# Attention probabilities: one exponential and a rounding copy on ACT, in place of two exponentials and some copies on DVE

## The chip, the core and the metric

The kernel runs on one core of one Trainium2 chip. The metric is the time of one launch in device microseconds; before the change the median of three runs is 2537.33 us (2531.2 to 2538.35). The engines are named as in the profile: PE is TensorE (matmul), with PEld for its weight loads; DVE is VectorE, ACT is ScalarE, POOL is GpSimd, SP is SyncE, which issues most of the DMAs. A row with `q` behind an engine's name (SPq) is that engine's sequencer.

## The reference, cut to what matters

Two layers, each a mixer with attention and a feed-forward block, on 1024 positions of width 1024, all in float32. Layer 0 has 12 causal heads of width 64 with a decay ("fox"), layer 1 has 12 causal heads of width 96 ("mla"); each layer adds 4 heads that look at 256 memory positions. In every head

```
logits = jnp.einsum('bhqd,bhkd->bhqk', qc, k).astype(jnp.float32)
logits = jnp.where(key_idx[None, :] <= q_idx[:, None], logits, -jnp.inf)
p = jax.nn.softmax(logits, axis=-1).astype(v.dtype)
return jnp.einsum('bhqk,bhkd->bhqd', p, v)
```

The probabilities `p` enter the second product. This is the place that the change touches.

## The kernel before, in words

PE multiplies values of the type float32r, which keeps fewer bits than float32. To keep the precision the kernel splits an operand into a high part (rounded to float32r) and a low part (the rest), and multiplies the parts apart. For the probabilities the high part is `ph`, the float32 value is `pf` and the low part `plo` is `pf - ph`.

Work goes head by head, and in a head by groups: a causal head has six groups of scores of 1024, 896 or 384 columns (two of each), a memory head has two of 1024. Each layer has 12 x 6 + 4 x 2 = 80 groups, the kernel 160. For each group:

- PE writes the transposed scores, with the row's maximum already subtracted by an extra row of the operands, into a PSUM tile `psS` (two buffers).
- `probs` turns them into `ph`, `pf` and `plo` (lines 329 to 341). In most groups ACT takes the exponential of `psS` twice, once rounded into `ph` (L335) and once in full into `pf` (L336). In every fifth group of layer 0 and every sixth of layer 1 (`pl.dve_turn`) ACT takes it once into `pf` (L338) and DVE rounds `pf` into `ph` (the helper `copy`, L85). POOL then subtracts (the helper `sub`, L90). `pf` has two buffers, `ph` and `plo` three.
- Two groups later PE multiplies `ph`, and one group after that `plo`, with the values (`av_units`), into the PSUM tile `psO` (one buffer). ACT copies `psO` out into `oh` (DVE does so for the memory heads of layer 0).

Beside this, PE, ACT and DVE prepare the next head: PE transposes into one of three `psX` tiles (L106), ACT scales them into `KA` and `QA` (L516), DVE makes the low parts `KB` and `QB` (L517), and DVE takes the maximum of a first pass over the scores (`mA`, L292 and L297), which PE also writes into `psX`. In layer 1 the queries and keys of a pair of heads are projected and normalised in the same stretch (`gq`, `gk`, `g_ss`, `rs_v`, `rs_y`, `rs_t` on DVE, `sq` and `rope` on POOL and DVE).

The code is not emitted in the order in which it runs. A scheduler that simulates the engines sets the order of each engine's list. In layer 0 it is free to move the matmuls of attention; in layer 1 they are pinned to the program's order (`pin[0] = not offset`), while ACT, DVE and POOL are free. All engines work through their lists in order, so an instruction that waits holds up all that stand behind it.

Of the kernel before, what the change touches and what calls it, by code (L numbers as in the profile page):

```python
# [11 lines left out]
AF = mybir.ActivationFunctionType  # L12
# [62 lines left out]
def hybrid_kernel(ctx: ExitStack, tc: tile.TileContext, A, out):  # L75
    nc = tc.nc
# [4 lines left out]
    def copy(eng, o, i):  # L81
        if eng == "a":
            nc.scalar.copy(o, i)  # L83
        elif eng == "v":
            nc.vector.tensor_copy(o, i)  # L85
        else:
            nc.gpsimd.tensor_copy(o, i)

    def sub(eng, o, a, b):
        (nc.vector if eng == "v" else nc.gpsimd).tensor_tensor(o, a, b, op=OP.subtract)  # L90
# [170 lines left out]

    pl = Pools()
    pl.mem_rows = set()
    pl.turn = 0

    def slot(name="slot", dt=F32):
        return pl.slots.tile([P, 1024], dt, name=name, tag="slot")
# [11 lines left out]
    def attention(L, heads, leads, offset=0, bg=None, fill={}):  # L279
# [30 lines left out]
        def score_units(h, g):  # L310
            half, parts = h.groups[g]
            state = {}

            def part(i):
                if i == 0:
                    state["ps"] = psS()
                ps = state["ps"]
                kt, q0, n, off = parts[i]
                passes = h.passes(kt, q0, n)
                for j, (l, r) in enumerate(passes):  # L320
                    mm(ps[:, off:off + n], l, r, j == 0, j == len(passes) - 1)
                if h.causal and q0 == kt * P:
                    mm(ps[:, off:off + P], idb, mS, False, True)
                if i == len(parts) - 1:
                    pend.append((h, g, *probs(ps, off + n)))

            return [lambda i=i: part(i) for i in range(len(parts))]

        def probs(ps, w):
            pf = pl.pf.tile([P, 1024], F32, name="pf")[:, :w]  # L330
            ph = pl.p.tile([P, 1024], F32R, name="ph")[:, :w]
            plo = pl.p.tile([P, 1024], F32R, name="plo", bufs=pl.nplo)[:, :w]
            pl.turn += 1
            if pl.turn % pl.dve_turn:
                nc.scalar.activation(ph, ps[:, :w], AF.Exp)  # L335
                nc.scalar.activation(pf, ps[:, :w], AF.Exp)  # L336
            else:
                nc.scalar.activation(pf, ps[:, :w], AF.Exp)  # L338
                copy("v", ph, pf)
            sub("p", plo, pf, ph.bitcast(F32))  # L340
            return ph, plo

# [134 lines left out]
    class Head:  # L477
# [6 lines left out]
        def qk_tiles(self):  # L484
            i = pl.nqk % len(pl.qk)
            pl.nqk += 1
            self.QA, self.KA, self.QB, self.KB = T = pl.qk[i]
            if self.causal and i not in pl.rows_set:
                pl.rows_set.add(i)
                for j, a, b in self.const_rows:  # L490
                    copy(self.rows_eng[len(pl.rows_set) > 1], T[j][a:b, :], ones1[a:b, 0:1].to_broadcast([b - a, S]))
# [873 lines left out]

    pl.split_out = split_out
    qk_tiles(qkp, (1, 2, 0), 3)
    pl.ev, pl.dve_turn = "v", 5
    fox = [FoxHead(h, QKV[h // 2][0], QKV[h // 2][1], cum) for h in range(NH)]
    mem = [MemHead(h, 0, mq0) for h in range(NMH)]  # L1370
    rest = attention(0, fox + mem, [2] * 16, offset=tc.cur_priority - p_last)
# [42 lines left out]
    with early(ffn.p_tail):  # L1414
# [4 lines left out]
        for d in range(ND):  # L1419
            raw = ffn.rp.tile([P, ND, P], F32, name="f_raw").rearrange("p a b -> p (a b)")[:, :N1 + N2]  # L1420
            nc.sync.dma_start(raw, mwin[d * P:(d + 1) * P, :])
            w = w1.tile([P, 2, N1 + N2], F32R, name="w1_w")
# [221 lines left out]
    def swap():  # L1644
# [3 lines left out]
        for p in (w1, xtp, hp):  # L1648
# [6 lines left out]

    fill = {2: [swap], 5: [lambda: g0.project(2)], 6: [lambda: latents_T(6)],
            10: [lambda: g0.project(3), lambda: g0.squares(1), lambda: g0.rotate(1), g0.scale_k, g0.scale_q]}
    pl.ev, pl.dve_turn = "a", 6
    mk = [slot("mK", F32R).rearrange("p (h i) -> p h i", h=NMH) for i in range(2)]

    ORDER = [12, 13, 14, 15, 0, 1, 2, 3, 4, 5, 6, 7, 8, 9, 10, 11]
# [98 lines left out]
```

## Time and profile before

| | us |
|---|---|
| median of 3 runs | 2537.33 |
| time of the profiled execution | 2535.55 |
| its span, first to last instruction | 2533.8 |
| attention of layer 0, stretch | 284 to 520 |
| attention of layer 1, stretch | 1397 to 1770 |
| PE busy in the span | 2372.8 |
| DVE busy in the span | 1905.2 |
| ACT busy in the span | 1208.7 |
| POOL busy in the span | 975.5 |

The two stretches are where `ph` is written and read (the first and the last use of it lie in them, with the preparation of the first head of layer 1). All else, the projections and the feed-forward blocks, holds no instruction of `probs`. Times of the rows below count from the start of the span.

### The profile page before, as it was taken

The page shows a single profiled execution, that of the slowest core. Times are in us where ns is not written, and L with a number is a line of the kernel's source. Part 1 is how long each engine was busy: PE and PEld are TensorE (multiplying, and loading weights), DVE is VectorE, ACT ScalarE, POOL GpSimd, SP SyncE. Part 2 cuts the span into 40 slices and gives each one's busy share as a digit, 9 for nine tenths or more (in the row PEclk, how much of TensorE's full clock was granted, in tenths as well). Part 3 has the DMA queues.
Part 4 walks back from the last instruction along what each step waited for, and adds up shares of the span by engine and source line. Part 5 has one row for each costly group of instructions (what it writes and reads, how often), then busy time and mean ns, then how long its engine had stood idle before and what let it go on. Part 6 is the DMA issues. An engine that isn't in the chain of part 4 may idle for free.

```text
span 2533.8 us, 32572 instructions
## 1 busy us (share of the span) xinstructions
PE 2372.8 (94%) x11609; PEld 1956.4 (77%) x11609; DVE 1905.2 (75%) x3289; ACT 1208.7 (48%) x2341; POOL 975.5 (38%) x640
## 2 busy tenths in 40 slices
PE   8999899988999999989998798989979999998999
PEld 7999666667788888868888576767768888886887
DVE  7432787737878877799997868874488778878998
ACT  5544678722544444434454555555144444443443
POOL 1122467732233333344322555666133233233442
PEclk9999899999999999999999899989999999999999
DMA  4221122262122222451230101011412222226221
GB/s 155 71 51 27 35 60 58 52 180 89 55 86 81 83 84 83 145 202 50 103 133 11 35 23 27 19 39 49 161 54 88 82 87 79 81 90 241 84 100 67
DMA packets 163652, 208.90 MB, mean 82 GB/s; under 512 B 11175, under 2 KB 124682, under 8 KB 163490
## 3 DMA queue, kind: packets, MB, share of 16 engines
q1 hardware_dynamic: 162054, 206.63, 25.9%
q8 instruction: 92, 1.51, 0.2%
q14 instruction: 70, 0.57, 0.1%
q10 hardware_dynamic: 1436, 0.18, 0.0%
HBM read 153.34 MB, written 39.98 MB: 76 GB/s over the span
## 4 chain that ended last, share of the span: by engine, by line
PE 71%; DVE 18%; DMA 4%; issue 3%; ACT 2%; POOL 1%; SPq 1%; DVEq 0%; ACTq 0%; POOLq 0%
PE psX L102 32%; PE psS L102 24%; PE psO L102 14%; DVE f_op L90 2%; DMA rrow<-rec 2%; PE psX L106 2%; DVE mA L292 1%; DVE psX L297 1%; DVE f_x L1134 1%; POOL f_op L90 1%; DVE rs_y L226 1%; DVE KB L517 1%; DVE QB L517 1%; DVE f_T L90 1%; DVE oh L93 1%
## 5 line engine op out<-in xcount | busy, mean ns | idle before, releaser
L90 POOL TENSOR_TENSOR f_op<-f_S,f_op 128x512 fp32r<-128x512 f32 x184 | 270.5, 1472 | 669.2 <-ACT f_op L83 612.0
L102 PE MATMUL psS<-f_T,f_op 128*128 128x512 f32 x1584 | 380.8, 391 | 5.4 <-DVE f_T L90 3.3
L90 POOL TENSOR_TENSOR plo<-pf,ph 128x1024 fp32r<-128x1024 f32 (+2 forms) x160 | 313.7, 1972 | 166.4 <-ACT pf L336 103.2
L102 PEld LDWEIGHTS psS<-f_T,f_op 128*128 128x128 f32 x1584 | 295.9, 188 | 66.9 <-DVE f_T L90 4.2
L102 PE MATMUL psX<-f_B,f_op 128*128 128x512 f32 x1260 | 296.3, 389 | 0.1
L83 ACT CAST f_op<-f_S 128x512 fp32r<-128x512 f32 x248 | 153.7, 621 | 279.5 <-PE psS L102 108.8
L102 PEld LDWEIGHTS psX<-f_B,f_op 128*128 128x128 f32 x1260 | 236.5, 188 | 49.6 <-issue 0.5
L102 PE MATMUL psS<-f_op 128*128 128x512 f32 x960 | 222.4, 390 | 0.4 <-DVE f_op L90 0.4
L102 PEld LDWEIGHTS psS<-f_op 128*128 128x128 f32 x960 | 180.6, 188 | 38.9 <-DVE f_op L90 1.2
L102 PE MATMUL psX<-f_op 128*128 128x512 f32 x666 | 174.5, 402 | 20.7 <-DVE f_op L90 18.0
L102 PE MATMUL psX<-w_w,hTh 128*128 128x384 f32 (+2 forms) x672 | 167.6, 334 | 2.2 <-ACT hTh L83 2.2
L102 PEld LDWEIGHTS psX<-f_op 128*128 128x128 f32 x666 | 127.3, 193 | 53.9 <-DVE f_op L90 24.4
L889 DVE SCALAR_TENSOR_TENSOR f_v<-f_cv,cw,f_v 128x1023 f32<-128x1023 f32 x88 | 151.0, 1715 | 7.6 <-ACT f_v L887 6.2
L83 ACT CAST f_op<-f_raw 128x512 fp32r<-128x512 f32 x148 | 91.4, 622 | 136.0 <-PE psS L102 70.7
L335 ACT ACTIVATE ph<-psS 128x1024 fp32r<-128x1024 f32 (+2 forms) x131 | 112.4, 858 | 89.6 <-PE psS L102 81.7
L102 PE MATMUL psX<-KA,QA 66*128 66x128 f32 (+4 forms) x320 | 111.4, 395 | 27.3 <-DVE mA L292 11.0
L83 ACT CAST f_op<-f_d 128x512 fp32r<-128x512 f32 x144 | 84.3, 619 | 102.0 <-PE psS L102 35.6
L849 DVE TENSOR_TENSOR f_u<-psS,f_p 128x512 f32<-128x512 f32 x44 | 30.4, 691 | 126.6 <-PE psS L102 126.6
L102 PEld LDWEIGHTS psX<-w_w,hTh 128*128 128x128 f32 x672 | 121.4, 190 | 3.3 <-ACT hTh L83 3.1
L102 PE MATMUL psS<-QA,KA 67*128 67x512 f32 (+7 forms) x304 | 111.4, 368 | 12.5 <-DMA QA<-mrow 12.4
L889 DVE SCALAR_TENSOR_TENSOR f_v<-f_cg,cw,f_v 128x1023 f32<-128x1023 f32 x88 | 112.7, 1280 | 10.9 <-ACT f_v L887 10.9
L90 POOL TENSOR_TENSOR f_op<-f_d,f_op 128x512 fp32r<-128x512 f32 x52 | 75.5, 1451 | 115.2 <-ACT f_op L83 115.2
(378 smaller groups left out, 5716.5 us busy)
## 6 DMA issues: line engine op xcount, KB each, us to landing
f_raw<-in_ffn_w_up_dram SPq DMA_DIRECT2D x88, 512.0 KB
g<-f_v SPq DMA_DIRECT2D x44, 512.0 KB
f_d<-g SPq DMA_DIRECT2D x36, 512.0 KB
f_d<-in_ffn_w_down_dram SPq DMA_DIRECT2D x36, 512.0 KB
w_raw<-in_fox_w_in_dram SPq DMA_DIRECT2D x48, 192.0 KB
rrow<-rec SPq DMA_DIRECT2D x32, 256.0 KB
wo_raw<-in_w_out_dram SPq DMA_DIRECT2D x32, 256.0 KB
xr<-x SPq DMA_DIRECT2D x16, 512.0 KB
```

The costliest lines, as they stand in the source:

```text
L83: nc.scalar.copy(o, i)
L90: (nc.vector if eng == "v" else nc.gpsimd).tensor_tensor(o, a, b, op=OP.subtract)
L93: (nc.vector if eng == "v" else nc.gpsimd).tensor_tensor(o, a, b, op=OP.mult)
L102: r = nc.tensor.matmul(*a, **k)
L106: r = nc.tensor.transpose(*a, **k)
L226: nc.vector.scalar_tensor_tensor(y, t, 1.5, y, op0=OP.add, op1=OP.mult)
L292: nc.vector.tensor_reduce(mA[:, q0:q0 + n], px[:, :n * width].rearrange("p (a b) -> p a b", a=n), axis=AX, op=OP.max)
L297: nc.vector.tensor_tensor_reduce(px[:, off:off + nk], px[:, off:off + nk], mQ[:, 512 - nk:], scale=1.0, scalar=m if on else NEG, op0=OP.ad ...
L335: nc.scalar.activation(ph, ps[:, :w], AF.Exp)
L517: nc.vector.scalar_tensor_tensor(Tl[tl0:tl1, hs], px, gcol, Th[0:n, hs].bitcast(F32), op0=OP.mult, op1=OP.subtract)
L849: nc.vector.tensor_tensor(o, x, y, op=OP.add)
L889: nc.vector.scalar_tensor_tensor(v[:, k:], src[:, :S - k], cw[:, 2 - k, ch:ch + 1], v[:, k:], op0=OP.mult, op1=OP.add)
```

## The change

`probs` takes one exponential into `pf` in every group, and ACT copies `pf`, rounded, into `ph`. The turn counter goes, and with it the copies on DVE. The later lines of the file move up by one to five: L335, L336 and L338 become L333, L516 becomes L511, L517 becomes L512, L297 becomes L296.

```diff
@@ -261,7 +261,6 @@
     pl = Pools()
     pl.mem_rows = set()
-    pl.turn = 0
@@ -330,13 +329,9 @@
             pf = pl.pf.tile([P, 1024], F32, name="pf")[:, :w]
             ph = pl.p.tile([P, 1024], F32R, name="ph")[:, :w]
             plo = pl.p.tile([P, 1024], F32R, name="plo", bufs=pl.nplo)[:, :w]
-            pl.turn += 1
-            if pl.turn % pl.dve_turn:
-                nc.scalar.activation(ph, ps[:, :w], AF.Exp)
-                nc.scalar.activation(pf, ps[:, :w], AF.Exp)
-            else:
-                nc.scalar.activation(pf, ps[:, :w], AF.Exp)
-                copy("v", ph, pf)
+
+            nc.scalar.activation(pf, ps[:, :w], AF.Exp)
+            copy("a", ph, pf)
             sub("p", plo, pf, ph.bitcast(F32))
             return ph, plo
@@ -1365,7 +1360,7 @@
-    pl.ev, pl.dve_turn = "v", 5
+    pl.ev = "v"
@@ -1655,7 +1650,7 @@
-    pl.ev, pl.dve_turn = "a", 6
+    pl.ev = "a"
```

Since a scheduler sets the lists, the change also moves other instructions. On PE the lists differ in the attention of layer 0 and in the last heads of layer 1; the feed-forward blocks and the first projections keep theirs. The first place is PE's list at the start of layer 0's attention, where `psS` takes the scores and `psO` the products with the probabilities of the first group:

```order
 L102 MATMUL psX<-KA_3076,QA_3075 128x512
-L102 MATMUL psO<-ph,vh 65x512
-L102 MATMUL psO<-ph,vl 64x512
-L102 MATMUL psO<-ph,vh 65x384
-L102 MATMUL psO<-ph,vl 64x384
+L102 MATMUL psS<-QB_3085,KB_3086 128x512
+L102 MATMUL psS<-QA_3083,KA_3084 128x512
+L102 MATMUL psS<-QB_3085,KB_3086 128x512
+L102 MATMUL psS<-QA_3083,KA_3084 128x512
 L102 MATMUL psS<-QB_3085,KB_3086 128x512
 L102 MATMUL psS<-QA_3083,KA_3084 128x512
```

The products of the first group with `ph` moved behind the scores of the next two groups.

The second place is ACT's list in layer 1, where a head's group of 896 columns falls beside the preparation of the next head (`KA_12777` and `QA_12776` are that head's operands). Before:

```order
L516 ACTIVATE QA_12776<-psX,g_cols 96x512
L335 ACTIVATE ph<-psS 128x896
L336 ACTIVATE pf<-psS 128x896
L516 ACTIVATE KA_12777<-psX,g_cols 96x512
L516 ACTIVATE QA_12776<-psX,g_cols 96x512
L338 ACTIVATE pf<-psS 128x384
```

And now:

```order
L511 ACTIVATE QA_12776<-psX,g_cols 96x512
L333 ACTIVATE pf<-psS 128x896
L511 ACTIVATE KA_12777<-psX,g_cols 96x512
L83 CAST ph<-pf 128x896
L511 ACTIVATE QA_12776<-psX,g_cols 96x512
L333 ACTIVATE pf<-psS 128x384
L83 CAST ph<-pf 128x384
```

The rounding copy stands behind `KA`, one instruction later than the second exponential stood.

The third place is DVE's list a little later in the same head, behind the low part `QB`, where the maximum over 128 columns is followed by the Newton steps of a norm (`rs_y`, `rs_t`). Before:

```order
L517 SCALAR_TENSOR_TENSOR QB_12778<-psX,g_cols,QA_12776 96x512
L297 ISA psX,mA<-psX,mQ 128x128
L297 ISA mA 128x1
L85 CAST ph<-pf 128x384
L217 TENSOR_SCALAR rs_y<-rs_v 128x16
```

And now:

```order
L512 SCALAR_TENSOR_TENSOR QB_12778<-psX,g_cols,QA_12776 96x512
L296 ISA psX,mA<-psX,mQ 128x128
L296 ISA mA 128x1
L217 TENSOR_SCALAR rs_y<-rs_v 128x16 x2
```

The copy is gone, and nothing took its place.

## Rows read from the trace of the kernel before

**Rows 1.** The page: chain that ended last, shares of the span by engine.
```profile
PE 71%; DVE 18%; DMA 4%; issue 3%; ACT 2%; POOL 1%; SPq 1%; DVEq 0%; ACTq 0%; POOLq 0%
```

**Rows 2.** Stretches: us, busy PE, PEld, DVE, ACT, POOL (instructions), clock, DMA, GB/s.
```profile
284.00:520.00 236.00, 216.49 (x1168) 156.64 (x1168) 186.33 (x357) 179.72 (x263) 170.23 (x90) 0.95 0.23 54
1397.00:1770.00 373.00, 327.01 (x1848) 253.29 (x1848) 274.66 (x615) 205.97 (x313) 227.67 (x148) 0.92 0.12 31
```

**Rows 3.** PE's longest wait for an engine, layer 0, then 1: us, times, longest.
```profile
PE psX L106 <- DVE mA L297: 8.3, 7, 2.2
...
PE psX L102 <- DVE mA L292: 9.2, 6, 3.9
```

**Rows 4.** Stretches as in rows 2, only instructions that touch the tile ph.
```profile
284.00:520.00 236.00, 73.39 (x308) 42.17 (x308) 14.14 (x16) 52.64 (x64) 155.26 (x80) 0.95 0.23 54
1397.00:1770.00 373.00, 85.85 (x320) 42.62 (x320) 7.83 (x13) 59.77 (x67) 156.03 (x80) 0.92 0.12 31
```

**Rows 5.** Groups of instructions by shape: busy us, mean ns, idle before and releaser.
```profile
L335 ACT ACTIVATE ph<-psS 128x1024 fp32r<-128x1024 f32 x56 | 57.3, 1024 | 45.7 <-PE psS L102 40.0 <-PE psO L102 5.4
...
L83 ACT CAST w_w<-w_raw 128x384 fp32r<-128x384 f32 x40 | 20.2, 513 | 24.2 <-DMA w_raw<-in_fox_w_in_dram 15.5 <-issue 8.0
...
L83 ACT CAST oth<-oh 128x1024 fp32r<-128x1024 f32 x12 | 12.6, 1050 | 16.2 <-DVE oh L93 16.2
```

**Rows 6.** DVE's copies into ph: count; ns least/median/most; first and last start; forms.
```profile
L85 DVE CAST ph<-pf x29: 342/622/2166, 300.9 to 1748.1; 128x384 fp32r<-128x384 f32 x16, 128x1024 fp32r<-128x1024 f32 x8, 128x896 fp32r<-128x896 f32 x5
```

**Rows 7.** Timelines of DVE, ACT and POOL in layer 1: start us, us.
```profile
1495.87 0.66 DVE L90 TENSOR_TENSOR gq<-rope 128x128 f32<-128x128 f32 x1
...
1508.69 0.92 ACT L335 ACTIVATE ph<-psS 128x896 fp32r<-128x896 f32 x1
1509.51 0.91 ACT L336 ACTIVATE pf<-psS 128x896 f32<-128x896 f32 x1
1510.30 0.68 ACT L516 ACTIVATE KA<-psX,g_cols 96x512 fp32r<-96x512 f32 x1
...
1510.50 2.10 POOL L90 TENSOR_TENSOR plo<-pf,ph 128x896 fp32r<-128x896 f32 x1 [0.17 <-ACT pf L336]
...
1511.15 1.60 DVE L90 TENSOR_TENSOR gq<-rope 128x128 f32<-128x128 f32 x1
```

**Rows 8.** ACT's timeline in the projections: one instruction waiting for the one before it.
```profile
201.39 0.21 ACT L231 ACTIVATION_READ_ACCUMULATOR junk<-psX 128x1 f32 x1
201.63 0.23 ACT L231 ACTIVATE junk<-psX 128x64 bf16<-128x64 f32 x1
```

**Rows 9.** Waits for ACT in layer 0's stretch: us in total, times, longest.
```profile
DVE QB L517 <- ACT QA L516: 3.0, 4, 1.7
DVE KB L517 <- ACT KA L516: 1.7, 4, 0.7
```

**Rows 10.** Chain of waits, pieces in both layers: start us, us on it, instruction.
```profile
399.31 1.42 DVE ph L85
...
417.54 0.55 DVE ph L85
...
427.18 1.57 DVE ph L85
...
478.46 0.81 ACT pf L336
...
1569.57 0.22 DVE ph L85
...
1675.73 2.04 DVE ph L85
```

**Rows 11.** Timelines of POOL and of DVE in layer 0: start us, us.
```profile
397.81 2.37 POOL L90 TENSOR_TENSOR plo<-pf,ph 128x1024 fp32r<-128x1024 f32 x1 [3.21 <-ACT pf L336]
...
399.18 1.55 DVE L85 CAST ph<-pf 128x1024 fp32r<-128x1024 f32 x1
```

**Rows 12.** A group of DVE in layer 0's stretch, columns as in rows 5.
```profile
L517 DVE SCALAR_TENSOR_TENSOR KB<-k,g_cols,KA 64x512 fp32r<-64x512 f32 x10 | 13.3, 1329 | 0.3
```

## The prediction

> **What bounds the kernel now.** I read the page's chain first, then the two attention stretches, and in them who waits for whom. The chain runs 71% on PE, 18% on DVE and 2% on ACT [rows 1], so time that leaves ACT or POOL counts only where PE or DVE was kept waiting. In the attention of layer 0 (236 us) PE is busy for 216.5 us, DVE for 186.3, ACT for 179.7; in that of layer 1 (373 us) PE for 327.0, DVE for 274.7, ACT for 206.0 [rows 2]. PE stands for 19.5 and 46.0 us, and the engine that it waits for longest in both is DVE: the maximum that has to be read before a `psX` buffer is free [rows 3]. ACT is a server with slack, more in layer 1 than in layer 0.
>
> **Part one: what leaves ACT and what comes to it.** 131 groups take two exponentials, 29 one and a copy on DVE (the count of `ph` on ACT in [rows 4] is 64 + 67, on DVE 16 + 13). In the 131 the second exponential of 1.024 us for 1024 columns becomes a copy from SBUF; the nearest copy of that shape took 1.050 [rows 5], so 0.026 more each, 131 x 0.026 = 3.4 us. The other 29 copies are new on ACT. They are 8 of 1024 columns, 5 of 896 and 16 of 384 [rows 6]; a copy of 384 took 0.513 [rows 5], one of 896 I estimate on the line between the two at 0.943: 8 x 1.050 + 5 x 0.943 + 16 x 0.513 = 21.3 us. And the copy needs the exponential that stands just before it in 91 of the 160 places in ACT's new list (30 in layer 0, 61 in layer 1). Two exponentials that follow each other start 0.82 us apart though the first took 0.92 [rows 7], that is, they overlap by 0.10; an instruction that waits for its forerunner starts 0.03 us after its end [rows 8]. So each of the 91 costs ACT 0.13, 11.8 us in all. Sum on ACT: 3.4 + 21.3 + 11.8 = 36.5 us, of which layer 0 has 64 x 0.026 + 7 x 1.050 + 5 x 0.943 + 4 x 0.513 + 30 x 0.13 = 19.7, so that ACT stands there at 199 of 236 us (84%, PE at 92%).
>
> How much of this reaches the end? ACT is idle for 56 us of layer 0's stretch. What others lose by waiting for ACT there is led by `QB` 3.0 and `KB` 1.7 us [rows 9]: 4.7 on 179.7 of work, 2.6%. Taking the same share of 36.5 gives +1.0 us. The ends are 0 (all behind ACT's waits for PE) and +19.7 (all of layer 0's growth seen); I take +1.0, since the row of waits measures just that share.
>
> **Part two: what leaves DVE.** 14.1 + 7.8 = 22.0 us of busy time [rows 4]. On the chain the copy appears at eight places; the rows show five, and 447.47 (0.53 us), 500.84 (0.60) and 1623.10 (0.21) are like their neighbours [rows 10]. Their sum is 1.42 + 0.55 + 1.57 + 0.53 + 0.60 + 0.22 + 0.21 + 2.04 = 7.1 us, the upper end. Not all of it is the copy's own. The copy at 399.18 stood for 1.55 us because POOL's subtraction ran from 397.81 to 400.18; it ended 0.55 us after that [rows 11]. Behind it stands `KB<-k`, which reads two SBUF tiles, and this form too takes 1.33 us in the mean [rows 12], 0.6 more than its twin from PSUM: it will wait for POOL in the copy's stead. So I count 0.55 there. At 1675.73 the next is `rs_y<-rs_v` in SBUF, which I treat alike, and count 0.22, as in the undisturbed place at 1569.57. At 427.18 the next is a maximum over PSUM, so all 1.57 go. Sum: 0.55 + 0.55 + 1.57 + 0.53 + 0.60 + 0.22 + 0.21 + 0.22 = 4.45. The lower end is 0, where what follows on DVE waits for PE anyway. I take -4.5.
>
> The Trainium skill ("SBUF — State Buffer", Who interferes with whom) says that a DVE copy in a two-port mode, or a DVE instruction with two SBUF inputs, shares a port pair with GpSimd, and that whoever issues second is blocked until the other is through. The trace agrees at 399.18. By this rule the sum is the 4.45 above; with the wait taken as the copy's own it would be 7.1. The skill also speaks against the change: "Perfetto Trace Analysis", Optimizing Scalar/DVE Operations, holds that a DVE mode makes such an operation faster than ACT, and that moving it pays where DVE is saturated. Here 29 copies took 22.0 us on DVE with POOL's blocking, and 21.3 are estimated on ACT, so the trace shows no such advantage left.
>
> **Part three: `psS` is free one ACT instruction earlier.** Now one exponential reads it, not two. PE's wait for the second is on the chain once clearly, at 478.46 for 0.81 us, followed by PE's scores [rows 10]: -0.8. The lower end is 0, since the exponential now first needs `pf`, which POOL frees. Against it stands that `ph` comes one instruction later. The new PE list answers this by putting `ph` products behind later scores, and there are two groups between.
>
> **Part four: who gets past whom in layer 1.** In four heads DVE's `gq<-rope` takes 1.60 us where it falls into POOL's subtraction for 896 columns (here 1510.50 to 1512.60, `gq` from 1511.15), and 0.66 where it does not [rows 7]; the other three are at 1565.95, 1619.46 and 1672.10. The subtraction will start later: one exponential (0.82), `KA` (0.68 less 0.10 of overlap) and the copy (0.94) put it at 1508.69 + 2.34 + 0.08 = 1511.11, 0.04 us ahead of `gq`. If POOL is still first, `gq` ends 0.6 later; if DVE is, 0.94 earlier: four times, +2.4 or -3.8. The 0.04 decides nothing, so I take 0.
>
> **Part five: the new list.** In layer 0 PE's list changes over the whole stretch. At best all of PE's 19.5 idle us go [rows 2], at worst as much again comes; the same planner made both lists, and I take 0.
>
> **Sum.** -4.5 - 0.8 + 1.0 = -4.3 us, on 2535.55 for the profiled execution: 2531.2. That execution is 1.8 under the median of 2537.33, so I forecast between the two bases, 2532. The least that a measurement of this kernel tells from no change is about 0.3%, 7.6 us, so the forecast itself is "no change that shows".
>
> **Rivals.** (1) ACT becomes the second bound of layer 0, and the kernel slower. Place: the end of each group there, where `QA`, `KA` and `oh` queue behind one more copy in every fifth group and a stall of 0.13 in others. For it: 84% on an engine that takes its work in order. Against: PE hardly waits for ACT now. Price: with all of layer 0's growth seen, 2535.6 + 19.7 - 5.3 = 2550.0. It decides as slower once two thirds of the 19.7 are seen (12.9 - 5.3 = 7.6).
> (2) DVE's relief is worth more than its places on the chain, because PE's longest wait in both stretches is for DVE: all 7.1 of the chain, 3.8 by `gq`, and 3 of PE's 19.5 idle us in layer 0 from 8.3 for `mA`: 2535.6 - 7.1 - 0.8 - 3.8 - 3.0 + 1.0 = 2521.9.
> (3) The copies only made room for waits that stand there anyway, and POOL stays ahead of `gq`: 2535.6 + 2.4 + 1.0 = 2539.0.
>
> **How the numbers follow.** Forecast 0.45, rival 1 0.22, rival 2 0.27, rival 3 0.06. Faster by over 0.3%: 0.24 of rival 2 and 0.06 of the forecast's lower edge, 0.30. Slower: 0.17 of rival 1, 0.01 of the forecast's upper edge, 0.02 of rival 3, 0.20. Within: the rest, 0.50. The forecast's own range, with `gq` either way and ACT's term up to 4, is 2526 to 2538. For 8 in 10 I go to 2520, a little past rival 2, and up to 2549, just short of rival 1.
>
> **What would show it.** The two attention stretches become shorter by 2 to 7 us in sum, all others stay within 1. No DVE row with `ph` is left; DVE's busy time falls by about 22 us, ACT's rises by 25 to 36. ACT's copy of 1024 columns takes about 1.05. PE's waits for DVE shrink, those for ACT stay under 3 us. In the four heads `gq<-rope` is either near 0.7 or over 2. I am wrong if layer 0's stretch grows, with PE waiting for ACT or for `ph`; or if the gain is over 8 us, with PE's idle time in layer 0 down by a quarter.

## The result: 0.6% slower, outside the stated range

The changed kernel takes 2557.24 us (median of 5 runs) against 2538.35 us for the kernel before, beside which it ran: 18.9 us between the medians, and a recorded ratio of 1.0063 with a 95% interval of 1.0046 to 1.0081 (12 to 21 us). The forecast was 2532, the range 2520 to 2549. The profiled execution took 2558.85 us, its span is 2557.1.

The chain of the changed kernel, shares by engine, answers to [rows 1]:

```profile
PE 72%; DVE 17%; DMA 5%; issue 3%; ACT 2%; POOL 1%; SPq 1%; DVEq 0%; ACTq 0%; POOLq 0%
```

The two attention stretches, columns as in [rows 2], with their ends moved to where the same work now ends:

```profile
284.00:533.00 249.00, 223.07 (x1172) 158.32 (x1172) 179.32 (x342) 196.57 (x279) 169.58 (x89) 0.93 0.22 51
1411.00:1792.00 381.00, 329.79 (x1851) 254.05 (x1850) 276.97 (x602) 220.97 (x327) 227.93 (x148) 0.92 0.12 30
```

Layer 0's stretch grew by 13 us and layer 1's by 8; everything between and behind them adds about 2. (That is one execution against one; how far a single stretch may be trusted is said with the experiments.) In layer 0 half of the growth is PE's idle time (19.5 to 25.9 us) and half is PE being busy longer with the same matmuls (216.5 to 223.1): the granted clock is at its lower level, 1.2 GHz, for more of the stretch, and the column shows a mean of 0.93 for 0.95. DVE, which lost 22 us of copies, is busy for 7 us less in layer 0 and for 2 us more in layer 1.

PE's longest waits in the changed kernel, layer 0 first, then layer 1 (columns as in [rows 3]):

```profile
PE psX L102 <- DMA KA<-cum: 6.6, 4, 3.1
PE psO L102 <- DVE oh L85: 6.1, 2, 5.8
PE psX L106 <- DVE mA L296: 5.6, 8, 1.3
PE psO L102 <- POOL plo L90: 2.2, 5, 0.6
PE psO L102 <- ACT ph L83: 1.4, 1, 1.4
```

```profile
PE psX L102 <- DVE QB L512: 7.8, 5, 1.8
PE psX L102 <- DVE mA L291: 6.4, 9, 2.8
PE psS L102 <- DMA QA<-mrow: 5.9, 2, 3.7
PE psX L106 <- DVE mA L296: 5.9, 3, 2.7
PE psX L106 <- POOL gk L93: 5.4, 3, 1.9
```

In layer 0 the first two waits are new. `KA<-cum` is a DMA that each head's preparation needs; under the new list PE reaches the head's first matmuls before it has landed. Both waits come again, at 6.9 and 6.1 us and at 7.2 and 4.7, in the two later runs that have this PE list in layer 0 (the change in layer 0 alone, and the changed kernel with `gk` on DVE). The 5.8 us for `oh` are one place, and the timelines of DVE, POOL and PE there (start us, us) show what it is made of:

```profile
517.50 4.72 DVE L93 TENSOR_TENSOR oh<-oh,rrow 128x512 f32<-128x512 f32 x2 [3.01 <-DMA rrow<-rec]
522.15 0.68 DVE L85 COPY oh<-psO 65x512 f32<-65x512 f32 x1
```

```profile
514.20 7.47 POOL L90 TENSOR_TENSOR plo<-pf,ph 128x1024 fp32r<-128x1024 f32 x3
```

```profile
522.88 0.69 PE L102 MATMUL psO<-ph,VHm 128*65 128x512 f32 x1 [5.78 <-DVE oh L85]
523.36 0.63 PE L102 MATMUL psO<-ph,VLm 128*64 128x512 f32 x1
```

Three subtractions of POOL stand in a row; DVE's two multiplications, 0.69 us each where nothing disturbs them, fall into them and take 4.72; the evacuation of `psO` queues behind, and PE, which has one `psO`, waits for it. It is a meeting of DVE and POOL at a bad moment.

### The profile page after: what moved, and what is told of

The parts are those of the page before. It is cut to its first block, busy times and chain, and to the rows that moved or that the text cites. A ratio compares the mean times of both kernels' runs of the same rounds, so it can differ in the third digit from the quotient of the medians.

```text
span 2557.1 us, 32700 instructions
## 1 busy us (share of the span) xinstructions
PE 2382.3 (93%) x11609; PEld 1959.8 (77%) x11609; DVE 1898.1 (74%) x3260; ACT 1240.2 (48%) x2370; POOL 978.2 (38%) x640
## 3 DMA queue, kind: packets, MB, share of 16 engines
q1 hardware_dynamic: 162054, 206.63, 25.8%
## 4 chain that ended last, share of the span: by engine, by line
PE 72%; DVE 17%; DMA 5%; issue 3%; ACT 2%; POOL 1%; SPq 1%; DVEq 0%; ACTq 0%; POOLq 0%
PE psX L102 32%; PE psS L102 23%; PE psO L102 14%; DMA rrow<-rec 2%; PE psX L106 2%; DVE f_op L90 1%; DVE psX L296 1%; DVE mA L291 1%; DVE oh L93 1%; DMA rec<-rec 1%; POOL f_op L90 1%; DVE rs_y L226 1%; DVE f_x L1129 1%; PE psS L106 1%; DVE QB L512 1%
## 5 line engine op out<-in xcount | busy, mean ns | idle before, releaser
L333 ACT ACTIVATE pf<-psS 128x1024 f32<-128x1024 f32 (+2 forms) x160 | 131.8, 829 | 81.9 <-PE psS L102 61.0
L83 ACT CAST ph<-pf 128x1024 fp32r<-128x1024 f32 (+2 forms) x160 | 135.8, 854 | 4.6 <-PE psO L102 1.7
```

## The experiments

Every ratio is to runs of the kernel before on the same chip; the ratios are those recorded with their intervals, and differ by up to about 0.1% from the quotient of two medians. "Layer 1's attention" is the time from the first to the last group's work there, 368.8 us in the profiled execution of before. Kernels whose layer 1 is that of before show 368.8 to 374.7 for it (seven executions), so single differences under 6 us say nothing. The 368.8 is the lowest of the seven and their median is 373.0: the changed kernel's 376.9 stands 8 us over the one and 4 over the other.

```profile
1399.40:1768.20 368.80, 322.81 (x1829) 249.76 (x1828) 271.96 (x611) 202.11 (x308) 224.99 (x146) 0.92 0.12 31
```

**One layer at a time.** `probs` takes the changed branch in one layer only:

```diff
+            if pl.layer == 0:        # second kernel: pl.layer == 1
+                nc.scalar.activation(pf, ps[:, :w], AF.Exp)
+                copy("a", ph, pf)
+            elif pl.turn % pl.dve_turn:
...
```

> The changed probabilities (one exponential over PSUM, ACT's copy from SBUF, no DVE copies) in layer 0's attention alone; layer 1 as before. The changed kernel's trace shows first products of the memory heads 10.2 us late and the end of layer 0's attention 13.8 us late, so every theory of layer 0 (new PE list; ACT's load; ph one ACT instruction later) expects +12 to +16 us against the kernel before, all of it before 660 us of the span, and layer 1's attention 371 us long as before. If instead layer 1's loss depends on what layer 0 left behind, this run shows the full +19.

Measured: 2553.96 us, 1.006 (1.0044 to 1.0077). PE's list in layer 0 is that of the changed kernel and the time up to the feed-forward block is 15.1 us longer, as there (13.8; in a third kernel with this list, the changed one with `gk` on DVE, 9.3). Eight executions with layer 0's list of before differ among themselves by up to 3.7 us at this point.

> The changed probabilities in layer 1's attention alone; layer 0 as before, with the same PE list there. Theory 'layer 1 loses by itself' (its PE list is that of the program in both kernels): +5 to +9 us, most of it in the first eight groups after 1397 us. Theory 'the changed kernel's loss is all of layer 0 and a shifted clock phase': within 3 us of the kernel before.

Measured: 2549.79 us, 1.0048 (1.0033 to 1.0063); layer 1's attention took 383.5 us, in an execution 4.4 us above that median. Both layers lose, each by itself; the two losses add up to 22.7 us in the medians, against 18.9 together. Layer 1's loss is not PE's list: that is the list of before up to the last heads, and where the two first differ (1742 us in the kernel before) layer 1 is already 13.4 us late.

**Is it the copy, the late `ph`, or ACT's load?** Two exponentials in all 160 groups, no DVE copies:

```diff
-            if pl.turn % pl.dve_turn:
...
+            nc.scalar.activation(ph, ps[:, :w], AF.Exp)   # second kernel: pf first
+            nc.scalar.activation(pf, ps[:, :w], AF.Exp)
```

> Two exponentials over PSUM in all 160 groups, ph first, no DVE copies: ACT gets 29 more second operations (about 21 us), DVE loses 22 us of copies, ph is as early as in the 131 groups before, and PE's list in layer 0 is about nine tenths that of the kernel before. Theory ACT load: most of the loss returns, +10 to +19 us. Theory late ph (ph comes one ACT instruction later and depends on it): within 3 us of the kernel before, or 4 us faster by the DVE term. Theory new PE list: also within 4 us of the kernel before.

Measured: 2554.74 us, 1.0063 (1.0038 to 1.0088).

> Two exponentials over PSUM in all groups, but pf first and ph second, no DVE copies: the same ACT work as with ph first, only ph comes one ACT instruction later, as in the changed kernel, without needing pf. PE's list in layer 0 is a third one. Theory late ph: layer 1 loses 5 to 8 us as in the changed kernel, layer 0 10 us or more. Theory ACT load: the same time as with ph first within 3 us in layer 1. Theory new PE list: layer 1 as before, layer 0 by its own list anywhere within 15 us.

Measured: 2550.68 us, 1.0045 (1.0028 to 1.0063). In their profiles layer 0 is not slower at all: up to the feed-forward block they stand 1.3 and 5.2 us ahead of the kernel before. The loss that they show is in layer 1 (381.8 and 381.3 us). The profiled executions took 2546.17 and 2545.63 us, 8.6 and 5.1 under the medians, so a part of the loss is not located. As far as they show, neither the 16 more instructions on ACT nor `ph` coming second costs layer 0 anything under these lists, and in layer 1 something is lost without the copy.

**The list of layer 0 held fixed.** PE pinned to the program's order there too, with four kinds of `probs` in layer 0 (before's, the copy, two exponentials, `pf` first), layer 1 as before. PE's list of layer 0 is the same in the first two; in the two with two exponentials it is the same until 554 us and differs behind that in the order of some matmuls of the output projection (`wo_w`).

```diff
-        pin[0] = not offset
+        pin[0] = True
```

> The kernel before with PE held to the program's order in layer 0's attention too (as layer 1's is in both kernels), two exponentials in four groups of five and DVE copies in the rest. It is the base for the next run. Its own time is not forecast by any theory; I expect layer 0's attention 5 to 25 us longer than the 239 us of the kernel before, the rest of the program unchanged within 5 us.

Measured: 2571.32 us, 1.0121 (1.0106 to 1.0137).

> The same pinned PE order in layer 0, word for word the same PE list, but with one exponential and ACT's copy in layer 0 (layer 1 as before). Theory new PE list (the loss of 13.8 us in layer 0 is the list's): layer 0's attention within 4 us of the pinned base. Theory late ph or ACT load (the instructions themselves): 10 us or more above the pinned base, with PE waiting for ACT's ph or POOL's plo.

Measured: 2579.47 us, 1.0155 (1.0139 to 1.0171).

> PE's order in layer 0 pinned to the program as in the two pinned kernels, and in layer 0 two exponentials over PSUM in every group, ph first, no DVE copies. Pinned, the change cost 5 us up to the start of the FFN (28.3 to 33.3 us above the kernel before). Theory ACT load (the seven copies of 1024, five of 896 and four of 384 that ACT took over): about the same 5 us. Theory late ph: within 2 us of the pinned base, or below it.

Measured: 2570.89 us, 1.0124 (1.0103 to 1.0146).

> The same with pf first: ph one ACT instruction later, but both exponentials read PSUM and none waits for the other. Theory ACT load: about 5 us above the pinned base, as with ph first. Theory late ph: 4 to 6 us above it, though ph first is not. Theory dependent copy (the stall between exponential and copy, and its price on ACT): within 2 us of the pinned base, in both orders.

Measured: 2566.63 us, 1.0116 (1.0091 to 1.0142). The stretches from the first score to the feed-forward block, in that order (columns as in [rows 2]):

```profile
280.70:671.90 391.20, 336.52 (x1631) 249.66 (x1631) 262.47 (x508) 209.71 (x313) 200.61 (x111) 0.92 0.27 75
```

```profile
281.00:676.90 395.90, 339.97 (x1632) 252.97 (x1632) 247.17 (x492) 229.39 (x329) 199.60 (x111) 0.90 0.27 74
```

```profile
280.70:671.00 390.30, 340.55 (x1632) 252.47 (x1633) 253.88 (x492) 221.43 (x329) 201.44 (x111) 0.91 0.27 75
```

```profile
280.60:672.30 391.70, 339.04 (x1633) 251.22 (x1633) 254.68 (x492) 221.38 (x329) 200.48 (x111) 0.91 0.27 75
```

Only the copy stands out: 4.7 us in the stretch, 8.2 between the medians. ACT has 329 instructions in each of the last three against 313 in the first, so their number is not it; ACT's busy time is 8 us higher with the copy (229.4 for 221.4). Of these, 2.5 us are the copies' own length and 5.5 are lost overlap, where the copy must wait for the exponential just before it: a pair of 1024 columns takes 2.10 us from start to end, two exponentials 1.94. The four rows also price what leaves DVE: without the 16 copies DVE is busy for 8 to 9 us less (253.9 and 254.7 for 262.5), and the stretch stays within 1 us, with the 16 exponentials that ACT takes over in their place (the medians are 0.4 and 4.7 us lower).

How the 13.8 us of layer 0 divide is an estimate, not shown by itself. Under the pinned order the instruction costs 4.7 us (8.2 in the medians), with 52 copies right behind their exponential; the changed kernel has 29 such places in layer 0. So about 5 us or less are the instruction, and the rest, about 9, goes with the list that the scheduler made for it. That a list alone can do this is seen in the next runs: with the copies two groups earlier layer 0 has another list, no work more, and is 6.7 us later at the feed-forward block (in an execution 7 us above its median).

**Is layer 1's loss a matter of place?** The kernel before with the same copies on DVE, but in other groups: counted two groups earlier in both layers, or one or three in layer 1 alone.

```diff
-    pl.turn = 0
+    pl.turn = 2
...
+    pl.turn += 1        # at layer 1's start alone; third kernel: 3
```

> The kernel before with the same number of DVE copies, one in five groups of layer 0 and one in six of layer 1, but two groups earlier in the count, so in other groups; all else equal. Theory place (what layer 1 loses is the meeting of DVE's norm chain with POOL's subtractions, which any move of instructions on DVE or ACT changes): layer 1's attention 6 to 15 us longer than the 371 us before although nothing was added or removed. Theory removal (layer 1 loses because 13 copies went to ACT): layer 1's attention within 3 us of before. In layer 0 PE's list is a new one, so by the theory of the list anything within 15 us.

Measured: 2555.76 us, 1.0056 (1.0038 to 1.0074), layer 1's attention 387.1 us.

> The kernel before with the copies on DVE in layer 1 one group earlier in the count (still one group in six), layer 0 untouched. Theory place: layer 1's attention anywhere from 0 to 18 us above 371, and not the same as in the next run. Theory removal: within 4 us of 371, since all copies are still on DVE.

Measured: 2545.21 us, 1.0025 (1.0015 to 1.0035), 383.0 us.

> The same, three groups earlier in the count. Theory place: again anywhere from 0 to 18 us above 371. Theory removal: within 4 us.

Measured: 2538.87 us, 1.0 (0.9991 to 1.0009), 373.8 us. The theory that the 13 copies had to leave DVE for layer 1 to lose has fallen: with all 13 still there and layer 0 untouched (the second of the three) the kernel is 6.7 us slower in the medians. The three are not free of other differences. The first and third have a 14th copy on DVE in layer 1, and in the last two twelve of the copies have 896 columns where before they had 384; DVE's copies there take 10.4, 8.1 and 10.4 us for 7.8. Place with these differences is worth from nothing to 17 us (of these some in layer 0).

What moved in layer 1 can be seen at the first step of the norm, `rs_v`, in the kernel before and in the second of the three (columns as in [rows 5]; in the third, which loses nothing, its mean is 452 ns):

```profile
L216 DVE TENSOR_SCALAR rs_v<-g_ss 128x16 f32<-128x16 f32 x12 | 3.4, 285 | 0.0
```

```profile
L216 DVE TENSOR_SCALAR rs_v<-g_ss 128x16 f32<-128x16 f32 x12 | 10.7, 889 | 0.0
```

**One suspected queue.** PE waits for POOL's `gk` in layer 1 for 2.6 us before, 5.4 in the changed kernel and up to 15.8 in the others. So `gk<-kr,rs_y` was put on DVE, in the changed kernel and in the one before:

```diff
-                mul("p", self.k[:, ts, :, 64:96], ...
+                mul("v", self.k[:, ts, :, 64:96], ...
```

> The changed kernel, with the second half of the key's scaling in layer 1 (gk<-kr,rs_y, 12 of 1.05 us on POOL) on DVE instead, so that it no longer queues behind POOL's subtractions of probabilities. PE's waits for POOL's gk in layer 1's attention were 2.6 us before, 5.4 changed, 8.0 with the change in layer 1 alone, 11.7 with pf first, 15.8 with the copies shifted. Theory gk (this queue carries layer 1's loss): that wait goes to 0 and layer 1's attention (379 us changed, 371 before) becomes 5 to 10 us shorter. Theory DVE chain (DVE's own blocked operations carry it): within 3 us of the changed kernel, since DVE gets 12 operations more.

Measured: 2559.21 us, 1.0078 (1.006 to 1.0095), layer 1's attention 377.7 us, against 376.9 without the edit.

> The kernel before with the same edit, gk<-kr,rs_y on DVE. Theory gk: only 2.6 us of waits are there to win, so layer 1's attention is 0 to 4 us shorter than 371, and the gap between this kernel and the changed one with the same edit is layer 0's 14 us alone. Theory place: any edit on DVE in layer 1 moves the meeting with POOL's subtractions, so 6 to 18 us longer.

Measured: 2547.51 us, 1.0027 (1.0015 to 1.0038), 374.4 us, within the range of the seven. The wait only changed its name, to DVE's `gk` (7.3 us in the changed kernel). That queue alone is not the carrier.

**POOL's long subtractions taken away.** In layer 1 POOL subtracts 128 columns only, and the low products read the high part; PE's work keeps its number and size. `probs` as before, with the copy, and with two exponentials:

```diff
+            if pl.layer == 1:
+                sub("p", plo[:, :P], pf[:, :P], ph[:, :P].bitcast(F32))
+                return ph, ph
```

> Leaves out part of the computation: in layer 1 POOL subtracts only 128 columns of each group's low part and the low products read the high part instead; PE's work is unchanged in number and size. Probabilities as in the kernel before. Theory meeting (DVE's small operations blocked for whole subtractions of 2.1 to 2.4 us carry layer 1's time): layer 1's attention 10 us or more shorter than 371. Theory ACT work: within 4 us of 371.

Measured: 2499.24 us, 0.9852 (0.9835 to 0.9869).

> The same with part of the computation left out, and the changed probabilities in layer 1 alone. With whole subtractions this pair was 9.2 us apart in the medians and 14.7 us in layer 1's attention. Theory meeting: the two are within 3 us of each other. Theory ACT work or dependent copy: 7 to 15 us apart as before.

Measured: 2505.73 us, 0.9869 (0.9854 to 0.9884).

> Leaves out part of the computation as the other two with shortened subtractions (128 columns of the low part in layer 1, low products read the high part). Two exponentials over PSUM in every group of layer 1, ph first, no DVE copies there. Theory dependent copy: layer 1's attention within 3 us of the 329.4 of the pair's base. Theory ACT's added work: 336 to 342 as with the copy.

Measured: 2511.19 us, 0.9894 (0.9879 to 0.9909). Layer 1's attention in the three (columns as in [rows 2]):

```profile
1401.40:1730.80 329.40, 302.95 (x1824) 237.86 (x1822) 224.86 (x611) 200.39 (x308) 112.69 (x145) 0.97 0.14 35
```

```profile
1400.60:1738.60 338.00, 312.17 (x1828) 244.29 (x1828) 227.96 (x599) 217.26 (x321) 112.19 (x146) 0.94 0.13 34
```

```profile
1400.70:1742.90 342.20, 311.27 (x1819) 242.49 (x1819) 223.29 (x598) 206.59 (x321) 114.47 (x145) 0.94 0.13 33
```

Without the long subtractions layer 1 is 39 us shorter, and DVE, with the same 611 instructions, is busy for 224.9 us where the kernel before has 272.0 in that stretch: 47 us of DVE's time were blocking. But the gap between the three stays in the profiles, against the theory of those subtractions alone: 8.6 us for the copy and 12.8 for two exponentials. For the copy it is not clear of noise: the medians are 6.5 us apart and the intervals overlap. The copy's 8.6 us are PE busy for 9.2 us more at a lower mean clock (0.94 for 0.97); its idle time is the same, 26.4 and 25.8 us. For two exponentials the trace shows one place. POOL's `gk` of the first kernel and of the third, in the same pair of heads:

```profile
1512.68 2.14 POOL L93 TENSOR_TENSOR gk<-kr,rs_y 128x256 f32<-128x256 f32 x2 [2.07 <-DVE rs_y L226]
```

```profile
1512.75 4.19 POOL L93 TENSOR_TENSOR gk<-kr,rs_y 128x256 f32<-128x256 f32 x2 [1.52 <-DVE rs_y L226]
```

DVE's scalings beside it, in the first and in the third:

```profile
1512.64 1.71 DVE L93 TENSOR_TENSOR gk<-gk,rs_y 128x512 f32<-128x512 f32 x2
1514.28 2.50 DVE L93 TENSOR_TENSOR gq<-gq,rs_y 128x768 f32<-128x768 f32 x2
```

```profile
1512.87 1.27 DVE L93 TENSOR_TENSOR gk<-gk,rs_y 128x512 f32<-128x512 f32 x2
1514.08 1.81 DVE L93 TENSOR_TENSOR gq<-gq,rs_y 128x768 f32<-128x768 f32 x2
```

And PE, which transposes `gk` next, again in the first and in the third, each with a stretch behind it that shows the clock (columns as in [rows 2]):

```profile
1513.86 0.64 PE L106 MATMUL psX<-ident,gk 128*96 128x128 f32 x4 [1.79 <-POOL gk L93]
```

```profile
1515.00:1521.00 6.00, 5.58 (x43) 4.86 (x43) 3.88 (x6) 4.24 (x8) 1.41 (x2) 1.00 0.00 0
```

```profile
1516.42 1.09 PE L106 MATMUL psX<-ident,gk 128*96 128x128 f32 x4 [3.73 <-POOL gk L93]
```

```profile
1515.00:1521.00 6.00, 4.58 (x17) 3.50 (x18) 2.10 (x4) 1.46 (x3) 2.35 (x3) 0.50 0.01 3
```

In the first kernel the two engines take turns. In the third DVE's four scalings go through undisturbed in 3.1 us and POOL's first `gk` lasts for all of them, 3.6 us where it otherwise takes 1.1. What it goes with is whether DVE's first scaling starts ahead or behind. In all runs together POOL's first `gk` takes 3.6 to 3.9 us in 20 places, and in each of them DVE starts 0.12 or 0.13 us behind it; in the 81 places where DVE starts with it or up to 0.05 ahead, it takes 1.12 to 1.15. PE waits 2 us longer and then goes on at 1.2 GHz, having stood still. This state of `gk` occurs three times each in both kernels with two exponentials and in this one, and four times in the one with the copies two groups earlier; in the kernel before and the changed one never. But it does not carry layer 1's loss everywhere: it occurs once in the first kernel here and once each in six runs whose layer 1 is that of before, and never in two runs that lose, the one with the change in layer 1 alone (383.5 us) and the one with the copies one group earlier (383.0).

**A version that beats both.** The shortened subtractions point to DVE's blocking, so the last run lets DVE do every third subtraction in layer 1 itself, with `pf` first in layer 0. That first half alone had been run:

```diff
+            if pl.layer == 0:
+                nc.scalar.activation(pf, ps[:, :w], AF.Exp)
+                nc.scalar.activation(ph, ps[:, :w], AF.Exp)
+            elif pl.turn % pl.dve_turn:
...
-            sub("p", plo, pf, ph.bitcast(F32))
+            sub("v" if pl.layer and pl.turn % 3 == 1 else "p", plo, pf, ph.bitcast(F32))
```

> A candidate: two exponentials over PSUM, pf first, in all groups of layer 0 (whose attention was 5 us shorter in the run that had it in both layers), layer 1 as before. If the two layers add: 4 to 6 us faster than the kernel before. If layer 1's part depends on the phase in which layer 0 leaves the engines: anything from 5 us faster to 5 us slower.

Measured: 2538.61 us, 0.9996 (0.9986 to 1.0005).

> A candidate: layer 0 with two exponentials, pf first; layer 1 as before, but DVE does the subtraction of every third group there, POOL the rest. If POOL's blocking of DVE (62 us of DVE's time in layer 1) falls by a third and DVE pays about 27 subtractions of 0.5 to 1.3 us: 0 to 10 us faster than before. If DVE's 275 of 371 busy us make it the bound: 5 to 15 us slower.

Measured: 2529.15 us, 0.9962 (0.995 to 0.9975), 9 us faster than the kernel before and 28 than the changed one. Its layer 1 and two of its groups there (columns as in [rows 2] and [rows 5]):

```profile
1396.70:1762.50 365.80, 318.81 (x1828) 246.67 (x1827) 284.07 (x638) 201.70 (x308) 176.43 (x119) 0.93 0.12 31
```

```profile
L90 POOL TENSOR_TENSOR plo<-pf,ph 128x1024 fp32r<-128x1024 f32 x17 | 40.7, 2396 | 69.7 <-ACT pf L339 49.2 <-PE psS L102 16.8 <-DVE ph L85 3.7
...
L90 DVE TENSOR_TENSOR plo<-pf,ph 128x1024 fp32r<-128x1024 f32 x15 | 18.4, 1229 | 4.8 <-ACT pf L339 4.8
```

DVE does a subtraction of 1024 columns in 1.23 us, POOL in 2.40 (of 384 columns in 0.90 and 1.01), and the 15 of these and 12 of 384 columns (10.8 us), 29.2 us of work, add only 12 us to DVE's busy time, which agrees with less of it being blocking. The gain of 9 us is clear of noise, but it stands on one choice of groups. Its layer 1 is 3 us under the lowest of the seven and 7 under their median, and other choices were not run, so how much of it is blocking saved and how much is place is not shown.

## Why the prediction was wrong, by its own steps

**Part one, ACT.** The sizes held. The changed kernel's copies of 1024 and 384 columns, columns as in [rows 5]:

```profile
L83 ACT CAST ph<-pf 128x1024 fp32r<-128x1024 f32 x64 | 66.7, 1047 | 1.2
...
L83 ACT CAST ph<-pf 128x384 fp32r<-128x384 f32 x48 | 24.6, 514 | 2.6 <-PE psO L102 1.7
```

1.047 and 0.514 were forecast at 1.050 and 0.513, a dependent pair costs 0.16 more, as forecast, and ACT's busy time grew by 31.5 us. What failed is the share that reaches the end: the row of waits for ACT gave 1.0 us, and the pinned pair shows 4.7 in layer 0 (8.2 in the medians). A share of waits measured under one load did not scale to instructions that lengthen each group's own path.

**Part two, DVE's relief: a step that failed.** -4.5 us were booked. Under the pinned order of layer 0, the copies gone from DVE shorten the stretch by less than 1 us, with ACT doing their work. (With `pf` first and a list of its own, layer 0 came out 2.8 to 5.2 us earlier in three kernels; whether that is this relief or the list is open.) The text said at two places that the next SBUF instruction would wait for POOL in the copy's stead; the other places were booked whole. Two groups of the norm in layer 1, changed kernel (columns as in [rows 5]):

```profile
L216 DVE TENSOR_SCALAR rs_v<-g_ss 128x16 f32<-128x16 f32 x12 | 10.2, 848 | 0.0
...
L217 DVE TENSOR_SCALAR rs_y<-rs_v 128x16 int32<-128x16 int32 x12 | 4.6, 410 | 0.0
```

Before they took 285 and 159 ns in the mean. In layer 1 7.8 us of copies left DVE, and its busy time rose by 3 us. It would go too far to say that these steps took over the removed copies' waits: with the copies one group earlier, and all still on DVE, they take 889 and 580 ns. What the change did was to move the moment at which they meet POOL.

**Part four, `gq` and POOL.** The good branch came true and brought no gain. `gq<-rope` is first in all four heads, at 0.27 us instead of 1.60, which was to give -3.8. DVE and POOL at one of them:

```profile
1585.59 0.28 DVE L90 TENSOR_TENSOR gq<-rope 128x128 f32<-128x128 f32 x1
1585.79 0.74 DVE L512 SCALAR_TENSOR_TENSOR KB<-psX,g_cols,KA 96x512 fp32r<-96x512 f32 x1
1586.45 1.44 DVE L216 TENSOR_SCALAR rs_v<-g_ss 128x16 f32<-128x16 f32 x1
1587.81 0.28 DVE L1473 TENSOR_TENSOR gq<-rope 128x128 f32<-128x128 f32 x1
1588.01 0.96 DVE L216 TENSOR_SCALAR rs_v<-g_ss 128x16 f32<-128x16 f32 x1
```

```profile
1585.63 3.31 POOL L90 TENSOR_TENSOR plo<-pf,ph 128x896 fp32r<-128x896 f32 x2 [0.86 <-ACT ph L83]
```

`gq` got past the subtraction, and the two `rs_v` behind it fell into it. A pair of heads takes 0.9 to 1.6 us longer than before (from one `gq` to the same one two heads on, 54.8, 53.5 and 52.6 us became 55.7, 55.1 and 54.1). The Trainium skill ("SBUF — State Buffer", Who interferes with whom) counts `tensor_scalar` among the operations that can take the port pair shared with GpSimd; 1.44 us for an instruction that takes 0.16 with the shortened subtractions agrees. By that rule the prediction had to follow POOL's subtraction down DVE's list, not to one instruction.

**Part five, the new list: the step that failed most.** 0 was taken, between -19.5 and +19.5, because one planner made both lists. That was no reason: two lists of this planner stood 6.7 us apart with no work added. The loss that goes with the list is about 9 us (13.8 less 4.7, the estimate above), and its two new waits, for `KA<-cum` and for `oh`, come in all three kernels that have it. The term was the largest of the sum and lay inside its stated bounds, but the final range did not reach them: it ended at 2549. For layer 1 the sum had no such term, only `gq` either way; there the change by itself cost 9 us in the medians.

**Part three**'s gain of 0.8 does not show: PE's wait for the exponential that frees `psS` was 0.4 us in layer 0's stretch and is 1.0.

**The rivals.** Rival 1 had the nearest time (2550), and half of its mechanism fell: 16 more instructions on ACT cost layer 0 nothing, pinned or not. Its other half, the stall behind the exponential, is the 4.7 us of the pinned pair. The prediction's own sign came half true: layer 0's stretch grew, but PE waits for ACT's `ph` there for 1.4 us and no more. (From the first score to the last product of layer 0 the chain lies on ACT for 28 us where it was 11, but for 17 to 22 also in the three kernels with `pf` first, which are not slower there.) That its time lay near is luck, since it knew no loss by the list and none in layer 1. Rival 2 fell with part two. Rival 3's first half, that the copies only made room for waits, agrees with the pinned runs; its second, POOL ahead of `gq`, fell. What decided was named in no rival: the list of layer 0, and the blocking of DVE and POOL falling on other instructions, at other moments, in both layers.

**What stays open.** The share of the list in layer 0 is known by subtraction alone. Why the clock goes down in more places of the pair with shortened subtractions, with the same idle time, was not settled; nor which single wait starts the loss in layer 1, since the rows show two forms of it (`gk` on POOL, `rs_v` on DVE) and taking `gk` off POOL did not remove the loss.

## What to carry to other kernels

Where two engines block each other, do not book the blocked time of an instruction that leaves: here the copies of layer 0 held DVE for 14 us, and their going shortened the pinned stretch by less than 1. When a change can move a scheduler's list or the phase of two such engines, run a control that moves the same instructions without removing any (copies in other groups, of the same size) before believing in a mechanism, and carry the full spread of that term into the range. The one version that gained shortened what blocks: a third of the subtractions on the engine that does the large ones twice as fast.

## What the runs showed of the hardware

POOL's multiplication of 1.1 us took 3.6 when four DVE multiplications with two SBUF operands ran back to back, as if it had to wait for all of them, though it started 0.12 us ahead of them in the profile (0.12 or 0.13 in all 20 places of the runs); with DVE's first 0.04 us ahead the two alternated. After a wait of PE of 3.73 us the granted clock stood at 0.50 (1.2 GHz), after one of 1.79 at the same place it stayed at 1.00, and the matmuls behind took 1.09 us for 0.64.
